# One decoder layer on one core: the written-out order of every engine and the engine of each free choice set anew

## The chip, the cores and the metric

The kernel runs on one core of a Trainium2 chip. The metric is device time in microseconds of one execution of the whole program, with all inputs and the output in HBM. A core has TensorE (PE in the profile; its weight loads are PEld), VectorE (DVE), ScalarE (ACT), GpSimd (POOL) and SyncE (SP), which here issues nearly all transfers. Each engine works through its own instructions in order; semaphores make one wait for another.

## The reference, cut to what matters

One layer of a decoder on a sequence of 512 tokens with 1024 channels, batch 1, all in float32:

```python
mod = silu(c) @ ada_w + ada_b                    # six rows of 1024: sh1, sc1, g1, sh2, sc2, g2
h = rms_norm(x, pre_norm_mix) * (1 + sc1) + sh1
z = h @ w_in                                     # g_rnn, x_rnn, q, k_c, v_c, k_s, v_s, k_w, v_w, gates
rnn = gelu(g_rnn) * rg_lru(causal_conv4(x_rnn))  # block-diagonal gates, then a scan over the tokens
att = nsa_attention(q, k.., v.., gates)          # compressed, selected and window parts, 8 heads, 2 KV groups
y = concat(rms_norm(rnn), rms_norm(att)) @ w_out
x = x + (1 + g1) * rms_norm(y, post_norm_mix)
h = rms_norm(x, pre_norm_mlp) * (1 + sc2) + sh2
y = square(relu(h @ w_ff1)) @ w_ff2              # 1024 -> 4096 -> 1024
x = x + (1 + g2) * rms_norm(y, post_norm_mlp)
```

## The kernel before

The float32 products are made of products of a shorter type: every operand is split into a high part (`hi`, a rounded copy) and a low part (`lo`, the operand minus `hi`), and three matmuls (hi x hi, lo x hi, hi x lo) are added up in PSUM. So each tile of weights takes, besides its load, a copy (`hi_a`, `hi_x`, `hi_g`, `hi_B`, `hi_e`, ...) and a subtraction (`lo_a`, ...) on ACT, DVE or POOL. The activations are split too (`h` and `h2l`, `fh` and `fl`).

The work goes in this order. First the four token tiles of `x` are normed and transposed, while the first sums of the modulation rows (`p<-p,silb`: a weight tile times the broadcast `silu(c)`, summed along the row) run on DVE. A first wave of projections makes keys, values and part of the rest. Then come the remaining projections, interleaved with the attention by blocks (scores `s`, masks and maxima `mx` on DVE, exponentials `p` on ACT, scaling by `den`, transposes `tp`, evacuation and split `pt`, products `pv`), with the recurrent block and with the projection out. From about 270 us on stands the MLP. Its first product (`up_pair`) and its second (`first_pair`, `second_pair`) use schemes in the manner of Strassen, with sums of weight tiles (`raw_A`, `raw_B`, `raw_D`) and of activations (`fS`, `fT`) ahead of the splits. The memsets of `K` (`zero`, L416) clear the half of each key tile that a head group does not use.

What sets the order is written out. While the program is built, every operation is a closure that the helpers `mm` (L340 in the profile), `turn` (L343), `act` (L350), `elem` (L384: DVE and POOL), `zero` (L416) and `load` (L430) append to a list of 5459 nodes. `flush` then sorts the list by a place for each node, two digits of the string `PLAN`, and calls it. So `PLAN` sets the order of each engine's queue and of SP's loads, and nothing else decides it. Where an operation can run on more than one engine (`copy`: ACT, DVE or POOL; `either`: DVE or POOL), a letter of `PLACE` (a, d, p) says which, taken in turn for each stream: XN norms of x, WS splits of weights and sums of weight tiles, AW after the first wave, AS scores, AV values, VW the recurrent block, FA end of the attention, RS residual, TH the transposed `h` of the MLP, UF and UP its first product, DN its second. There are 1056 letters.

```python
at = [b * DIGITS.index(PLAN[2 * k]) + DIGITS.index(PLAN[2 * k + 1]) for k in range(n)]
for k in sorted(range(n), key=at.__getitem__):
    self.nodes[k]()
...
ways = [w for w in ways if w[0][0] == PLACE[self.name][k]]
```

The tiles `fh` and `fl` of the second product lie in the pool `an` (L1687), in memory that the tiles of the pool `h2p` (`h2`, `h2l`, `s4h`) used before. Three neighbouring pools and `h2p` itself are opened with `reuse_waits="tile"`, `an` is not.

Of the kernel before, what the change touches and what calls it, by code (L numbers as in the profile page):

```python
# [14 lines left out]
P = 128  # L15
S = 512
D = 1024
# [48 lines left out]
    '&O&5&`&@&<&F&Q&J&f&U&=&G&p&M&l&e&H&N%z%d%y%u%{%}&+&9&4&L&0&>&]&v&[&o&g&q&R(-&b&{&h&t&S(/&c(#&k(F&T&P'
    '&7&K&.&C&E&I&_&X&i&,&D&m(1&s(%&x(H&z(;(2()&y(T(<(>(C(*&|(V(?#/(E(@(Q(L(.(3(8(=($(()%)*+2%X(|(h)2):(B'
    '(P(K(U(R(Y(a(~(G(6)3)9)>)U)b)y)^(m*2*8+l*d)/)C*A*K+d*o&a&*&u%q&V&Y(:&?(+&j(t&~)n(4)H(D*h(y*J)|*v*$+7'
    ')s+,*r+S+++x+&,<*),V,n#d#+#f#2$))?&d&n(&(5(7&w&r&}(,(W([#:#=#@#C#E#H#J#R#S#W#Y#[(9(A(I(j(Z(g(v#`#a#b'
    '#g#j#l#o#p(J(M(N#r#>#w$%#z(O(S(X(^(i(n(x(z({(})#)$)&)))0)Z)4)A)J*#*C+r/((](_(`(b(c(d(e(f(r)()M(k(l(o'  # L70
    '(p(q(s(u(w)G)Y)x)+),)-).)6)7)8)<)O)d)p)F)I)K)N)P)Q)R)S)W)v*+*5)a)e)h)1)5);)=)@)B)D)E)L)T)V)X)[)])_)c'
    ')j)o)t)w)z)~*%*(*F***4*t)`)f)g)i)k)l)m)q*T*]*y)r)u){)}*&*,*.*/*N*V+/*1*6*7*9*:*;*<*>*p+A+T*3*@*D*E*G'
    '*I*L*M*O*P*Q*S*U*W*X*Y*Z*_*`*b*c*i*j*k+:+)+L+G+E+[+o*a*l*m*w*x*{*|*}+#+i,4,>+0+4+8*[*^*e*-*0*?*=*H*B'
    '+?+F+M+N+|+u,),1*f*g*n*q*s*u*z*~+%+(+*+-+1+6+9+;+<+C+H+I+J+z,?,G,Z+Q+R+U+V+W+X+Y+]+`+b+e+h+k+m+n+s+t'
    '+v,,,6,8,;,=,C,F,M.P.q,Y,{-A.H+~,#,$*R+$-y.8,&,*,/,`,g-6/O,0,3,5,@,A,B,D,E,I,J,L,N,O,f,h,m,o,p,s,w,}'
    '-&+.+3+B+w+@,%+D+K+=+>+c+f+j,7+a+q-*-/-2-8-?-:-C->-1,P,R,S,U,[,b,c,e,j,k,l,q,r,t,u,v,x,y,z,|,~-#-$-%'
    '-+-J-P-V-(-)---.-0-3-5-7-9+O+P+^+}+Z,-+_,2-;-<-=+p+{,(,a,+,d,.,:-,-4-O-d-T-K-^-R-Y-@-B-D-E-H-M-N-Q-W'
    '-Z-c-q.$.5.:/&-F-S-U-]-b-m-I-L-X-f-_-`-e-h-j-l-u-x-|.t0%0K+g+y,T,i,Q,X.*.,.0,9,H,K-G.>.?.@.C.E.F/D/b'
    '/}.G.I.K.N.Q.`.e.k/>/M/80>0H#m.#.&.(.1.;.<.J.a.d-z.2.3.9.=.O-o-w.M.W,W,]-k-v-a-p,^,_-[-i.%.).x.{.4./'
    '...B.V.Z.].f.g.h/0/c/J-r-s.+.R.-.D-g-n-t-{.X.Y.b.c/%/..j.l.m.s/+/5.6.7._.i.[.n-}-~.A.U.v.|/_/#/F///g'  # L80
# [1813 lines left out]
```

## Time and profile before

| | |
|---|---|
| median of 3 runs | 605.06 us (604.8, 605.06, 607.66) |
| span of the profiled execution | 603.6 us; its own time is not listed |
| PE busy | 578.5 us, 96% of the span, 3424 matmuls |
| DVE busy | 562.5 us, 93%, 1148 instructions |
| ACT busy | 417.9 us, 69%, 848 |
| POOL busy | 193.7 us, 32%, 196 |
| chain that ended last | PE 75%, DVE 16%, ACT 4%, issue 2%, DMA 2% |
| HBM | 86.35 MB read, 2.10 MB written, 147 GB/s over the span |

The profile is of one execution. "L384 DVE" is an instruction that the helper at line 384 put on VectorE; since all share few lines, tiles are told apart by names: `out<-in`, with shapes behind. "x2" is a count; "[1.42 <-DVE mx L384]" is the idle time of the engine before an instruction and what ended it. Matmuls are pipelined and their ends are modelled, so a busy PE is not always at its rate.

### The profile page before, as it was taken

The numbers are of one execution on the slowest core, as the hardware profiler recorded it, in microseconds if no ns is written. First come the engines' busy times: TensorE is split into PE (matmuls) and PEld (weight loads), VectorE is DVE, ScalarE is ACT, GpSimd is POOL, SyncE is SP. The second block draws the span as 40 slices with busy tenths as digits, with TensorE's granted clock in tenths as the row PEclk, the third lists the DMA queues.
The fourth block names the chain that finished last, engine by engine and source line by source line (L and its number), as shares of the span: only waits on it lengthen the run. The fifth ranks groups of instructions, "written<-read, shape, count | busy, mean of one in ns | idle before, by whom it ended". The sixth has DMA issues, their size and how long they took to land.

```text
span 603.6 us, 9935 instructions
## 1 busy us (share of the span) xinstructions
PE 578.5 (96%) x3424; PEld 504.0 (84%) x3424; DVE 562.5 (93%) x1148; ACT 417.9 (69%) x848; POOL 193.7 (32%) x196
## 2 busy tenths in 40 slices
...
GB/s 347 416 377 372 280 283 181 36 75 100 6 275 175 71 47 61 1 105 71 71 141 140 72 140 73 138 130 189 222 54 151 128 157 122 147 168 123 121 1 139
DMA packets 26977, 89.08 MB, mean 148 GB/s; under 512 B 2992, under 2 KB 3504, under 8 KB 26928
## 3 DMA queue, kind: packets, MB, share of 16 engines
...
q14 instruction: 22, 0.18, 0.1%
...
HBM read 86.35 MB, written 2.10 MB: 147 GB/s over the span
## 4 chain that ended last, share of the span: by engine, by line
PE 75%; DVE 16%; ACT 4%; issue 2%; DMA 2%; POOL 0%; DVEq 0%; ACTq 0%
PE f L340 24%; PE pv L340 18%; PE s L340 17%; PE tp L340 11%; PE tp L343 4%; DVE r L384 4%; DVE p L384 3%; DVE fT L384 2%; DMA ar<-in_ada_r 1%; DVE raw_A L384 1%; DVE lo_c L384 1%; DVE lo_B L384 1%; ACT junk L350 1%; DMA vecs<-in_vecs 1%; DVE pt L384 1%
## 5 line engine op out<-in xcount | busy, mean ns | idle before, releaser
L350 ACT ACTIVATE p<-p,mx 128x32 f32<-128x32 f32 (+4 forms) x96 | 45.2, 473 | 10.2 <-DVE mx L384 10.1
L384 POOL TENSOR_SCALAR p<-p,den 128x32 f32<-128x32 f32 (+4 forms) x49 | 46.5, 964 | 13.6 <-DVE p L384 6.0
L340 PE MATMUL f<-hi_o,h 128*128 128x512 f32 x128 | 46.2, 410 | 0.2 <-ACT h L350 0.2
L350 ACT ACTIVATE hi_B<-raw_A 128x512 fp32r<-128x512 f32 x34 | 21.5, 633 | 29.1 <-DVE raw_A L384 14.9
L343 PE MATMUL tp<-ident,p 128*128 128x128 f32 x192 | 36.3, 273 | 1.1 <-DVE p L384 0.9
L340 PE MATMUL pv<-pt,V 128*128 128x256 f32 x160 | 36.8, 310 | 0.5 <-DVE pt L384 0.3
L384 DVE TENSOR_TENSOR pt<-tp,pt 128x512 fp32r<-128x512 f32 (+1 forms) x56 | 33.6, 609 | 3.6 <-ACT pt L350 2.1
L340 PE MATMUL s<-K,Q 128*128 128x288 f32 (+4 forms) x128 | 34.1, 330 | 1.4 <-DVE mx L384 1.4
L350 ACT ACTIVATE fT<-fT 128x512 f32<-128x512 f32 x52 | 31.5, 623 | 5.6 <-DVE fT L384 5.1
L384 DVE CUSTOM_DVE_ANT_0 p<-p,silb 128x1024 f32<-128x1024 f32 x24 | 31.2, 1308 | 0.1
L340 PEld LDWEIGHTS pv<-pt,V 128*128 128x128 f32 x160 | 26.2, 189 | 5.2 <-DVE pt L384 1.8
L350 ACT ACTIVATE pt<-tp 128x512 fp32r<-128x512 f32 (+1 forms) x47 | 25.3, 542 | 6.1 <-PE tp L343 4.2
L343 PEld LDWEIGHTS tp<-ident,p 128*128 128x128 f32 x192 | 24.3, 140 | 5.4 <-issue 1.7
L340 PEld LDWEIGHTS f<-hi_o,h 128*128 128x128 f32 x128 | 23.0, 188 | 4.1 <-ACT h L350 0.6
L340 PEld LDWEIGHTS s<-K,Q 128*128 128x128 f32 x128 | 22.2, 190 | 4.8 <-DVE mx L384 1.9
L340 PE MATMUL f<-lo_o,h 128*128 128x512 f32 x64 | 25.7, 403 | 0.0
L350 ACT ACTIVATE junk<-r 128x1024 bf16<-128x1024 f32 (+2 forms) x21 | 18.0, 856 | 10.7 <-DVE r L384 10.6
L340 PE MATMUL f<-third,hi_B 128*128 128x256 f32 x96 | 23.4, 283 | 0.9 <-DVE fT L384 0.9
L384 POOL TENSOR_TENSOR lo_e<-t,hi_e 128x512 fp32r<-128x512 f32 x1 | 1.3, 1297 | 67.4 <-ACT hi_e L350 67.4
L384 DVE TENSOR_TENSOR lo_B<-raw_A,hi_B 128x512 fp32r<-128x512 f32 x30 | 20.6, 687 | 2.4 <-ACT hi_B L350 0.9
L340 PE MATMUL f<-h,hi_g 128*128 128x512 f32 x64 | 22.5, 401 | 0.0
L340 PE MATMUL pv<-r,hi_B 128*128 128x256 f32 x96 | 22.2, 285 | 0.2 <-DVE fT L384 0.2
...
## 6 DMA issues: line engine op xcount, KB each, us to landing
...
```

Source lines behind the costliest of these rows:

```text
L340: lambda: self.nc.tensor.matmul(out, lhs, rhs, start=start, stop=stop))
L343: self.issue("pe", 0.109, [out], [src], lambda: self.nc.tensor.transpose(out, src, ident))
L350: return "act", cost, lambda: self.nc.scalar.activation(out, src, func, scale=scale, bias=bias, **kw), func
L384: return eng, cost, lambda: fn(out, *args, **kw), None
```

## The change

The set of operations is the same. The string `PLAN` is replaced as a whole (all queues and the loads get another order), 167 of the 1056 letters of `PLACE` differ, and the pool `an` gets `reuse_waits="tile"`, with which the first use of a tile waits for those older tiles that lay in its own memory, and not for the whole earlier pool. In the making of the new strings, an instruction of VectorE and one of GpSimd on SBUF were taken as excluding each other.

By letters: DVE to POOL 47, ACT to POOL 19, POOL to DVE 29, POOL to ACT 15, ACT to DVE 36, DVE to ACT 21. The core of the diff (`PLAN`, about 110 lines of digits, and the rows of `PLACE` for WS, UP and DN, 759 letters in all, of which 85 differ, are left out):

```diff
 PLACE = {'': 'aa',
-         'XN': 'aaadaaaaaaaa',
+         'XN': 'paaaaaaaaaaa',
...
-         'AW': 'aaaaaaaadpppadadddppadad',
-         'AS': 'papaaaappppaappppapappppdpaaddpaddpdpaaapapaapppppppaapappdpadapapaadadpppapappapppppppppppppadd'
-          'ppppapapdpaaapap',
-         'AV': 'aaaaaadaadadadaaaaaaadadadadaaaaaaaaaaaaaaaaaaaaaaadaaaa',
+         'AW': 'aaaaaaaaddppadadddppadad',
+         'AS': 'ddpaapappppppppdaapaadaapppapppppddpppaapappapppppapaaapdpaappppdadaaappppppdpappappdapdapppaapa'
+          'dpdppaadppapapap',
+         'AV': 'aadaaaaaddaaaaaaaadaadddddadadaaaaadaaaadaaaaaadaaadaaaa',
...
-         'FA': 'pppppdppdddp',
-         'RS': 'ppdppaddaddd',
-         'TH': 'aappaadddaddaaddaaddaaddaaddaadddaddaddaddaddddd',
-         'UF': 'adad',
+         'FA': 'ppppppppppdd',
+         'RS': 'pppppaddaddd',
+         'TH': 'aappaapddadddaddaappadddaappaadddaddaddaddaddddd',
+         'UF': 'addd',
...
-    an = ctx.enter_context(tc.tile_pool(name="an", bufs=1))
+    an = ctx.enter_context(tc.tile_pool(name="an", bufs=1, reuse_waits="tile"))
```

What the order does at the places spoken of below: the two evacuations `Q<-f,Q` that now stand behind sums `p<-p,silb` at 85 us stand ahead of three of them; the sum `ar<-ar,silb,ab` that is at 120.18 us in the trace goes 21 places back in DVE's queue, behind splits `pt`, and two `eg` go later; the two memsets of `K` leave the beginning of POOL's queue and stand around `lo_x` (one between `hi_x` and `lo_x`, one three instructions behind); the load of `raw_x` before them is issued three places earlier; a compressor weight's load goes from 12th to 35th; PE's eight products with `sil` come ahead of its ten warm-up products, of which four stood among them.

More of the change, by code (lines that the diff above doesn't have):

```diff
@@ L66 @@
[L66 to L80, printed above, removed]
@@ L166 @@
[L166 to L170 removed]
+    '#%#.#p#/#0#8#=#E#,#2#6#7#F#N#P#Q#S#e#L#M#O#R#d#*#(###$#&#)#+#b#U#c#x#K#T$$$%$&$($)$*$+$,$-#-#Y#Z#]$2'
@@ new lines @@
+    '$Y#5#^#_#g#i$[#V#`#a#h$5$8#f#n#v#{$7$h#t#o#q#y$:$.$/$0$1$4$3$6$>#w$<#z#|$;$I$F$k$H$N$R$J$G$l$Q$O$T$r'
+    '$i$m$j$o$V$?#~$#$`$=$K$L$P$U$W$X$a$9$A%9${$p$n$t$q$x$|$s$z$u$w$y%$$}%#$~%A%($B#}$@$_%7$D$E$M$S$]$^$e'
+    '$Z$d%Q%%%@%&%)%J%F%.%B%C%G%L%T%1%E%D%H%Y%U$C$b$c%6%5%+%-%/%0%2%3%<$g%;%P%Z%M%X%I%b%V%]%[%i%_%c%^%n%r'
+    '%p%m%o%a%=$f%:%O%8$v%*%,%K%R%S%e%4%>%N%s&?%x%q&<%k&8&D&5&6&>&;&9&G&7&:&E&@%?%f%h%j%l%t%u%y%{&)%z&&&/'
+    '&=&M&Q&B&F&A&L&O&R&C&X&N&[&Y&S&V&Z&P%|%d%g%W%`%v%w%~&$&+&%&-&k&s()&q&]&z&W&t(*&u&^(.&r&}(3&y&v(/(#&('
@@ new lines @@
+    '%}&,&H&I&J&K&U&`&d&#&*&l(+(E&{&w(0(,(-(F&|&x(D(1(4(K&~(((G(2#W(9(8(=(C(%($(:(5(6(7(|(Z,<&.(V(T)6)8(&'
+    '(?(;(S(A(B(X)#(<(>)&)()>)U)@)V(Y(U)A*B+Y*N*(.@*%*@+V*G&a&3&h&2&e&0&b&1&g&j)$&p)h):*D*+*K&n)W*,*M)}*I'
+    '*T+4*S+5*R+o+M,5-6,u-^#X,~#[*P&4))&T&c(H(I(J&i&_&f&m(@([#1#3#4#9#:#;#>#?#@#A#B#C(L(M(N(}(W(~)9#D#G#H'
+    '#I#J#j#k#l(O(P(Q#m#<#s+3#u(R(](^(_(`(a(b(c(d(e(f(g(j(p)+*&({)7);*E*J.9/A(h(i(k(l(m(n(o(q(z)%)<(r(s(t'
+    '(u(v(w(x(y)=)S)f)*)-)/)0)1)2)3)4)?)T)e)5)K)L)N)O)P)Q)R)X)d)g**)^)_)c),).)B)C)D)E)F)G)H)I)J)M)Y)Z)[)]'
@@ new lines @@
+    ')`)a)b)i)k)l)o)p)~*#*)*U)j)m)n)q)r)s)t)u*?*F*Q)v)w)x)y)z){)|*-*$*C+O*.*/*0*3*4*5*6*;*O+,+L*1*2*<*=*>'
+    '*V*W*X*Y*[*]*b*e*f*g*h*i*k*l*m*o*t*w*z*}*|+.+-+7+P,;*Z*j*n*q*r*s*u*v*{+_+s,>*~+#+6*9*:*^*7*8+8*A+T*H'
+    '+9+?+G+`,.,k,w,t*_*`*a*d*p*x*y+$+%+&+(+)+*+:+;+<+=+>+A+B+K+[,3,4,=+@+D+H+I+a+b+c+d+e+f+g+h+i+l+m+n+u'
+    '+v+w+z+{+|+}+~,,-#.2/|,9,:-Z-c+t+x+y*L+2.8.e,#,(,*,p,|.c/H,@,A,B,C,D,E,F,G,H,I,J,K,L,M,N,O,P,R,j,},l'
+    ',o*c+++1,m+0,0+/+Z+C+J+S,n+W,/+X,2,q,r,s,v-4,x,y-$,z,?,Q,S,T,U,W,X,Z,[,],_,`,a,b,c,d,e,f,g-&-.-/-0-1'
@@ new lines @@
+    '-3-9-L-]-:-<-=->-?-@-A-Q-R+E+F+R+^+U,-+Q+]-S-T-U+j+k+p,++r,1+q,{-5-7-8-E-e-F-C-D-f-V-i-j-k-l-n-q-t-u'
+    '-v-y-z.4.G.=/t-%-)-*-2-G-Y-(-;-K-b-m-o-}.#.%.&.-.../.[/I/},$,),6-H,8-I.0.H.I,%,&,7,i.J.K.L.M.N.O/G/s'
+    '/~.P.R.T.U.V.W.Z.d.Y0u.~0A3x#r-O-h.(.).+.,.7.D.a-x-{-|.*.E.F-p.$.?.^,^,h-,-J---N,V,Y-+-M-d-g.`/*.>.1'
+    '.5.3.X.f.g.p.v/#/-/=/J-B-X-`.6-_.A-P-W-[-a.o.q.r.s.{/(.h.i.u.w/+/@-w-~.:.B.<.C-r-s.;.].|.}/h/,/./0//'
+    '/C/4/9/:/;/1/6/D/F/</P/Q/T.Q.S.b/K._/M.j.k/)/f/[/]/e0t1y/R/V/Y/Z/d/r/W/X/^/k/x/y.t.x/?/a/>/B/7/8/E/L'
@@ new lines @@
+    '/u/v0r0p0&0%/w/z/o0)0+0500010?0@060D0F0G/_/g/O/b0H0I0]0l0j0E0J0K0N0b0s070M0O0P0a0y0*0:/p0$131415161&'
+    '1(1;1>1m1z1L1O1P1R1%1K1i1t0C0^2<2=2>2?2@2A2B3K440,0<1$1+1#1)0m0n101/0;/c0_0(0=090`.l.m.n0>121A11/$/%'
+    '/&1@0o0}0B/2/3/50q1F1E1B1D1e1}1d1f/N/S/U1I1J1_1g2L2h/`/i/j1|/l/m/n/q0-022I03040L080k3w1C.y.z0.0/0Q0R'
+    '0S0T0U0V0W0X0Y0Z0[0c0d0e0f0g0h0i0v0w0{0z0~1*0x0|3u1W1[1]1o21252627282;2O2P2Q2R2S2T2U2V2X2Y2_2`2a2b2p'
+    '2}3J3y171?1G1j1c1l1,1-1.1~18191:1M1N1Q1S1T1V1Y1Z1^1p2,2-1r1s1{2&1u2$1<1=1H1h2*2+2G3#2C2E2F2e2.2/201n'
@@ new lines @@
+    '1q1x2D1v2(1w2)2223241U1X1`2#1a2%1b1k2H2k2n3$4%3S3Q2~3U2s2t2x3]4{5&5h3+3,3-2W2Z2[2^2f2m2q2r2u2v2{3(35'
+    '36372N2]2i2y2l2z2j2|292:2K2c2J2d2M2g3%3)3*3O3R3[4y4i4>383;3<3A3B3F3H3I3`3a3b3d3e3h3i3m3n3o4#5V6D7A3&'
+    '3_3N4$3M3}3T4)3Y3p4&492w3.303:3Z3r3=3>3?3@3^3t3C3D3E3G3/333P3X4/4041434*4:3~4<4(4=4A4@4B4c4d4e4f4j4o'
+    '4p3{5f&o/{+N3q0#2o3|4I4M4z5W5^3k3l4-4.46484r4s4|5#34393L513V5A31323W5C4+4,424J4K4R4T4U4V4X4g4q524;4C'
+    '4E4F4Y4Z4[4G4N4`4a4k3z4h4l5X4n4L4O4S4W5b5i4~5,5n6q6+5(5)5*5+5B5`4w4}5.5a3f3g3s4?475@3c3j454x5Z5]5e6w'
@@ new lines @@
+    '5o5d6N5c4]4^4_4b4t4u5358595Q5R5S5t5u5z5{5|5}5~615s5w5y6%6,6#6$646:6G6?6@6C6L6K6&65686;6F6H4P4Q5/6/5-'
+    '5D6T6U6W6^6r6s4D4H4v5?6u6v7#7$7%54555E6a6h6i6j6X6Y6e6f6t6~56575<625=5k5F5I5J6y7?6A6p:/7&7)7+747(7*7-'
+    '7>5$5%50636E6I6J6M6}6|7L7M5M5N5O5P5T5U5l7J7R6{7O:.6=6P6Q6R6S6b6c6g6k767@7k8r77787=7]5K5L5Y6.5_5m6l6m'
+    '6n6z7_7`829,9*5:5;5>5j7B7W7Y7Z7m7n5x6(6667696<6V6[6]7U7V7a7b7o7p5q5v6)6-6*606_6`6d6x737C7X7[7^7f7x7y'
+    '7{5G5H5[6B6O6o8s8t7N7j887T8#8$8%868(8)8*8;7u7v7}7~858P8<8=8>8?7|8&8S8T6>6Z7/7K7.7H5p5r7,7I7071727579'
@@ new lines @@
+    '7:7q7t818A>S7D7E7g7h7i7w803v:-4m5g8O8V8z:>>R8C8D8G8L8X8[8^8b8c8k8v8u8W8Y8]8_8j8p8`8e8f8g8w9(7;7G7S7s'
+    '7Q7r7<7F7P7l8-8.8{9V878q838/8H8n8|9%90929S9l9o:q8K8d8h8~9K9a:,:2:F:H:I:J:V919394969#9&9?9C97989=9D7c'
+    '7e8@8M7d7z8,848+9F9J9Y9x:?9/95999;9@9O9H9I9L9R9]9`898:8B8N8E8F8Q8i9M9c9d9g9b9j9y9|9h9n:%:&8I8J8R8x8U'
+    '8Z8a8o8y9.9A9X9Z9B9W9[9U:*:+:7:A:@8}9$9-9v8l8m9+9>9)9r9~:#:$:6:=:0:3:4:5:9:S:Z:R:g:h:i9:9<9N9u9E9G9P'
+    ':8:K:N:O:]:C:E:L:M:[:p:b:d:e:m:^:_:`:a:j:s9Q9T9^9t9_9e9f9m9w:::X;/;|;.;-;3;M;#;2;J;[;D9s:;;K;L:u:x;$'
@@ new lines @@
+    ';%:w:y;I;O;&;9;;;Q9p9q9};,9i9k9{:Q9z:f:k:o:t:v:|:~;8;C;r<+<5<C:{;:;<;=;>;q<2<I<J;R;T;Z;^;c;d;l<-;p;@'
+    ';A;B;V;a;b:(:):<:P:1:G:W;0<e<f<u=+;f;g;h;i;m;o<Q<{<|<}=@=P;s;x;y;z;t;u;v;w;}</:B:D:T:Y:U:l:n:r;1;4;5'
+    '<W;_;{;H;P;X=k=m=r=t=u=v=}<&<(<)<*;~<#<$<%<0<1<,<6<7<8<3<4<<<D:c:z:};E;);*;6;G;7=w>(>)>*>+>,>->.>/>0'
+    '>1>2>9<9<@<A<K<L<S<T=<<d<=<><?<B<F<U<M<N<O<P<a<b;(;+;N<H;?;S;U<;<R<Y<_<g<Z<[<]<^<`<i<h<j<l<t<k<m<n<o'
+    '<r=*;W;e;n<:<.;j;k<E<G<V<c=5=&<q=%<s=(<v<w<x<~<y<z=$=,=#=-=2===>=B=^=a=`=.=/=0=1=;=E=?=A=C=D=F=H=G=I'
@@ new lines @@
+    '=N=O=J=K=L=M=R=Z=W=X=Y=[=S=T=U=V=_=b=]=d=f=g=c=e=h=i=l=n=o=p=q=s=x=z=y=|>#>4=~>$>3>8>W>Z>:><>[>7>F>Q'
+    '>6>G>T>]>c>d?/?Y@.?)@->e>g>m@/>n>o>p>~>C>D>^>_>`>a>|?$?|?~@I@J@N@i@K@M@k>b>f>h>i>j>l>};F;`<X;];Y<p=)'
+    '=4=6=Q=3=8=9=:=7=j={>%>&>5>=>A>B>E>J>P>O>N?0?1>;>>>?>@>M>H>K>L?2>y>k>q>u>x?*?,?(?%?9?:>r>s>t>w?-?+?#'
+    '?.?X?{>v?;?A?B?C?F?J?O?P?Q?[?a?b?j?k?l?n?o?p?q?v?w@<@C>I>U>V>Y>X?<?=?>???@?D?E?R?]?^?_?`>z>{?3?6?d?e'
+    '?f?g?h?r?t?u?x?y@1@U?s?z@%@&@(@*@+@0@2@4@5@6@7@@@A?}@B@D@W@X@Y@Z@q@s@v?&?4?5?8?7?T?i@Q@R@S@T@]@^@m?W'
@@ new lines @@
+    '?Z@$@)@n@t@u@x@z@{A$A%A?ATAUAZA]B,B@@,@8@9@:@;@F@G@H@E@L@w@3@=@>@?@d@e@O@P@lA4@_@`@a@b@h@f@g@cA3A2A)'
+    'A,A-A.A/AGA1A0A6AJA7A9ADA8AHAMAEAIALANAPB1A5AOB3B0@[@|A*A;A<A=ASA[A^A_A`AaAbAcAdAhAsAtAvAwAxAyB%B)@V'
+    '@o@p@rA(A:A>A@AAABAeAfAgAiAjAkArAuB&B(B+B-B.B/@y@}@~A#A&A+ACARAVAWAXAYAlAmAnAoApAzA{A|A}A~B#B$BABBBG'
+    'BHBIBJBKBVBWBZB[B]B_B`BaBbBdBeBhBkBlBmBnBq@#B4@jAFAKBrBsC.DKAQB5B2B6B:B=B9B>B;CUB7DADHOsB8C4CYCuCxCy'
+    'DJMbC/?G?H?I?K?L?M?N?S?U?V?c?mB<BMBTBYBcBfBgBiBjBtBvBwB|B?BEBFBLBNBOBPBSBUBXB^C,C2BQBRBuBxByBzB}C(C:'
@@ new lines @@
+    'C=CACHCZBoBpC#C$C&C*C+C<C?C@CBCGC[C^AqB*BCBDB{B~C%C>CCCDCECMCqCrCzDBC)CFCICJCKCNCOCPCQCRCSCTCpCsD@DC'
+    'G}C-C0C1C5C6C7CXC_C3CVC]CWCwCoCtCvC`CaDMDIC8C9C;CLCdCeCfCmD&D(D)D*DED+D,D6DPDoDpDqDrDsDtDvDwCbCcCnC{'
+    'C|C}C~D#D$D/D1D4DFCjCkD;DSDTDUDXDYDZD[D]D^DjCgChCiClD%D5D7D8D9D:D>D?DGD|D=DNDQDRDVD_D`DaDbDcDdDhDlD}'
+    'E,FfD-D.D0D2D3D<DODWDeDfDgDnE*E^F`FyM3DyE&E(E-E.E0E[EbE+E/EaDiDkEcEdEfDmDxF(F&E4E7E:E;E=E>E?EEEGEHEI'
+    'EKE]EFEJELEPEQEREUEVEWEXEYEZElEmEnEoEpErEtEvEwEzF#F%F)DuDzD{D~E#E$E%E)E1E2E5E6FBESETEqEsEuExEyE}F*F.'
```

160 lines of the change are left out of this document (57 added, 103 removed).

## The prediction

> **What bounds the kernel now.** I read the page's busy line and chain first, then TensorE's waits, then tables by stretch, and last the order of time around each wait.
>
> ```profile
> span 603.6 us, 9935 instructions
> PE 578.5 (96%) x3424; PEld 504.0 (84%) x3424; DVE 562.5 (93%) x1148; ACT 417.9 (69%) x848; POOL 193.7 (32%) x196
> PE 75%; DVE 16%; ACT 4%; issue 2%; DMA 2%; POOL 0%; DVEq 0%; ACTq 0%
> ```
>
> Two engines are nearly full: PE (TensorE) carries 75% of the chain that ended last, DVE (VectorE) 16%, POOL (GpSimd) 0%. The same matmuls run afterwards, so what an order can win is the time in which PE stands, or runs under its rate.
>
> ```profile
> PE s L340 <- DMA r<-in_x: 4.8, 1, 4.8
> PE s L340 <- ACT h L350: 1.8, 1, 1.8
> PE pv L340 <- DVE pt L384: 1.5, 2, 1.1
> ...
> PE s L340 <- ACT fh L350: 0.2, 1, 0.2
> ```
>
> After the first load (4.8, which no order removes) the waits are short and few (columns: total, times, longest); most of the others follow further down with the rows around them, and they are for DVE. Next, stretches: length, then busy time of PE, PEld, DVE, ACT and POOL, granted clock, DMA share, GB/s.
>
> ```profile
> 80.00:90.00 10.00, 8.27 (x46) 6.16 (x44) 9.75 (x18) 4.42 (x8) 9.84 (x3) 1.00 0.78 292
> 90.00:100.00 10.00, 9.33 (x41) 7.95 (x42) 8.70 (x30) 5.48 (x23) 1.04 (x2) 0.83 0.47 190
> 150.00:270.00 120.00, 118.66 (x723) 102.21 (x722) 112.04 (x313) 109.87 (x281) 84.50 (x93) 1.00 0.27 93
> 210.00:240.00 30.00, 30.00 (x201) 27.08 (x200) 28.39 (x103) 27.98 (x76) 23.75 (x30) 1.00 0.15 54
> 270.00:570.00 300.00, 298.36 (x1868) 268.94 (x1869) 288.55 (x498) 187.56 (x322) 47.98 (x40) 1.00 0.38 128
> 480.00:510.00 30.00, 30.00 (x134) 24.68 (x133) 29.83 (x47) 20.56 (x33) 0.00 (x0) 1.00 0.43 139
> ```
>
> From 270 to 570 PE idles 1.6 us of 300: what can be won lies ahead of that, where PE waits (80 to 90: 8.27 of 10) and where the clock drops behind a wait (0.83 from 90 to 100). Around four of the waits stand these rows.
>
> ```profile
> 80.07 3.77 POOL L384 TENSOR_SCALAR hi_x<-raw_x 128x1024 fp32r<-128x1024 f32 x1 [16.38 <-DMA raw_x<-in_wcol]
> ...
> 83.31 0.29 PE L340 MATMUL s<-K,Q 128*128 128x288 f32 x1
> ...
> 83.92 3.32 POOL L384 TENSOR_TENSOR lo_x<-raw_x,hi_x 128x1024 fp32r<-128x1024 f32 x1
> 84.92 3.40 DVE L384 CUSTOM_DVE_ANT_0 p<-p,silb 128x1024 f32<-128x1024 f32 x1
> 89.13 1.39 DVE L384 SCALAR_TENSOR_TENSOR Q<-f,Q 64x512 fp32r<-64x512 f32 x2
> 89.16 0.53 PE L340 MATMUL s<-K,Q 128*128 128x288 f32 x2 [1.42 <-DVE mx L384]
> 90.67 0.70 PE L340 MATMUL f<-h,hi_x 128*128 128x512 f32 x2 [0.99 <-DVE Q L384]
> ...
> 123.22 0.41 PE L343 MATMUL tp<-ident,p 128*128 128x128 f32 x2 [0.91 <-DVE p L384]
> 123.26 2.38 POOL L384 TENSOR_TENSOR lo_g<-raw_g,hi_g 128x1024 fp32r<-128x1024 f32 x1
> 123.40 2.27 DVE L384 TENSOR_SCALAR eg<-eg 128x24 f32<-128x24 f32 x1
> 126.72 0.38 PE L340 MATMUL pv<-pt,VC 128*128 128x256 f32 x1 [1.14 <-DVE pt L384]
> ...
> 268.51 3.10 POOL L384 TENSOR_SCALAR hi_f<-raw_f 128x1024 fp32r<-128x1024 f32 x1
> 268.88 1.60 DVE L384 TENSOR_TENSOR h2l<-h,h 128x256 fp32r<-128x256 f32 x2
> 270.20 0.39 PE L340 MATMUL pv<-h2l,hi_f 128*128 128x256 f32 x1 [0.34 <-DVE h2l L384]
> ...
> 403.14 1.30 POOL L384 TENSOR_TENSOR lo_B<-raw_B,hi_B 128x512 fp32r<-128x512 f32 x1 [8.44 <-ACT hi_B L350]
> 403.32 1.67 DVE L384 TENSOR_TENSOR raw_A<-raw_A,raw_B 128x512 f32<-128x512 f32 x1
> 405.93 0.35 PE L340 MATMUL f<-third,hi_B 128*128 128x256 f32 x1 [0.92 <-DVE fT L384]
> ```
> ```profile
> L384 DVE CUSTOM_DVE_ANT_0 p<-p,silb 128x1024 f32<-128x1024 f32 x24 | 31.2, 1308 | 0.1
> L384 DVE TENSOR_SCALAR eg<-eg 128x24 f32<-128x24 f32 x4 | 2.8, 708 | 0.1
> L384 DVE TENSOR_TENSOR lo_B<-raw_A,hi_B 128x512 fp32r<-128x512 f32 x30 | 20.6, 687 | 2.4 <-ACT hi_B L350 0.9 <-issue 0.4 <-PE pv L340 0.4
> L384 DVE TENSOR_TENSOR fl<-fS,fh 128x256 fp32r<-128x256 f32 x36 | 14.8, 417 | 0.0
> L384 POOL TENSOR_TENSOR lo_B<-raw_A,hi_B 128x512 fp32r<-128x512 f32 x6 | 8.1, 1348 | 19.4 <-ACT hi_B L350 19.4
> L384 POOL TENSOR_TENSOR fl<-fS,fh 128x256 fp32r<-128x256 f32 x4 | 4.8, 1192 | 18.1 <-ACT fh L350 18.1
> L384 POOL TENSOR_TENSOR fS<-fT,fT 128x256 f32<-128x256 f32 x4 | 3.3, 824 | 3.6 <-ACT fT L350 3.6
> L384 POOL TENSOR_SCALAR hi_g<-raw_g 128x1024 fp32r<-128x1024 f32 x1 | 2.8, 2767 | 0.0
> ```
>
> Each time a DVE instruction overstays beside a POOL instruction on SBUF: `p` 3.40 against a mean of 1.31, the 24 columns of `eg` 2.27 where the three others take (2.8 - 2.27) / 3 = 0.18, `raw_A` 1.67 against 0.69 for a row of its size. `eg` ends at 125.67 with POOL's `lo_g` at 125.64. So POOL shuts DVE out, but not always: from 210 to 240 DVE is busy 28.39 and POOL 23.75 of 30, where DVE mostly reads scores in PSUM.
>
> **The change part by part.** The diff adds and removes no operation; engine letters at 167 of 1056 choices and the whole order differ, and one pool's waits. So I compared the two orders of each queue.
>
> *80 to 100.* Now two sums `p` stand in DVE's queue ahead of both `Q` evacuations, so one `p` held by `lo_x` makes PE wait 1.42 + 0.99. In the new order both `Q` stand ahead of three sums. The wait goes: 2.4. The clock at 0.83 for 10 us costs 10 x 0.17 = 1.7, and goes with it if the idle caused it (from 0 to 1.7; I take 1.7, as the stretch before it stood at 1.00). Late next: the first maxima `mx`, one instruction behind `Q`.
>
> *120 to 127.* The sum `ar` at the head of this group moves 21 places back, behind the `pt` splits, and `eg` back too; the waits 0.91 and 1.14 go: 2.05. Against it, three copies `hi_g` come to POOL, 2.77 each, and one `hi_v`; that is within the +29 below.
>
> *270 and 406.* That `hi_f` leaves POOL: 0.34. That `lo_B` leaves POOL for DVE, 0.69 there, which is less than the hold of 0.98; the wait 0.92 may go or be met by its own `lo_B`: half, 0.46.
>
> *The beginning.*
>
> ```profile
> 4.65 1.25 POOL L416 MEMSET K<- 64x1056 f32 x1
> 5.11 0.82 DVE L384 TENSOR_SCALAR sil<-sil 128x8 f32<-128x8 f32 x1
> ```
>
> The two `K` memsets leave the head of POOL's queue, so `sil`, 8 columns, can take what the 24 of `eg` take, 0.18: 0.64 earlier. All eight silb matmuls come before the ten warm-up matmuls, but PE's first real matmul waits 1.8 for ACT's `h`, whose norm also waits for the fourth tile. From 0 to 1.0; I take 0.7. The `K` memsets don't vanish: one now stands between `hi_x` and `lo_x`. `hi_x` waits for its load and ends at 83.84; with 1.25 behind it the memset ends at 85.1, and scores from that `K` began at 83.31. So the cost is 0 to 1.8. The load of `raw_x` is issued three places earlier, ahead of two of 512 KB, which at 292 GB/s take 1.8 each; so I take 0.5, for `lo_x` coming later too.
>
> *`reuse_waits`.* The pool of `fh`/`fl` then waits for the tiles it overlays one by one. ACT's `fh` waits for matmuls now, and PE for `fh` 0.2: from 0 to 0.6, as ACT has 31% free; I take 0.3.
>
> *Engine letters.* 66 instructions come to POOL and 44 leave it. At the mean of the nearest row each: 256 wide with two inputs 21 in, 8 out, at 0.82 to 1.19 (+11 at 0.86, as `fS` is the commoner); 512 wide with two inputs 11 in, 5 out, at 1.35 (+8); 1024 wide copies 5 in, 2 out, at 2.77 (+8); 1024 wide with two inputs 2 in, 1 out, at 2.38 (+2); softmax scalings and other small work 27 in, 28 out, about even. Net +29 on 193.7. DVE gets 65 and gives 68: -2.9. ACT: -11.5, off the path with 31% idle. Of POOL's +29, 11 fall in 270 to 420 and 11 behind it, where DVE gives 1.6 and 5.0.
>
> What do the added 29 cost? POOL has room; DVE may be held. The four rows above lose 2.1 + 2.1 + 0.8 + 1.0 = 6.0 on DVE for 193.7 of POOL, so 29 at that rate lose 0.9. From -0.9 (new pairs all better placed) to all 29 held; I take double the rate, 1.8, since most lands where DVE is fullest, and 0.5 more for waits that a shuffled PE order opens at places with none now.
>
> *Queues.* SP's loads: the first eleven stand almost as before, one compressor weight goes from 12th to 35th. At 512 KB each and 292 GB/s, 35 loads take 63 us, so it is there before the scores at 83.31, and its product is formed beside them. PE's order moves by seven places on average; ACT's table loads keep their number and sequence.
>
> Sum: 2.4 + 1.7 + 2.05 + 0.34 + 0.46 + 0.7 + 0.3 = 7.95, less 0.5 + 1.8 + 0.5 = 2.8, leaves 5.15. The span goes from 603.6 to 598.5. The median before, 605.06, is 1.46 above that span (runs 604.8 to 607.66; the profiled execution's own time isn't given), so I forecast 605.06 - 5.15 = **599.9**. A difference under 0.5% (3 us) a measurement of this kernel can't tell from none.
>
> The Trainium skill, "SBUF — State Buffer", section "Who interferes with whom", says that a VectorE instruction with two SBUF inputs, or in a two-port mode, and a GpSimd instruction that reads SBUF exclude each other for a whole instruction, and that the one issued first decides. The ends of `eg` and `lo_g` within 0.03 agree; so do the PSUM readers from 210 to 240. By the page every added POOL instruction beside DVE's two-input splits is a hold, which speaks against the new letters: it would give the third rival's 609 in place of my 599.9.
>
> **The rivals.**
>
> *No change (602 to 608).* The holds move to other places and PE, 96% busy, keeps its pace: the 7.95 come back as other short waits. For it: PE is at 30.00 of 30 in the quietest stretches; the six waits are 1% of the span. Against: each is a DVE instruction standing ahead of one that PE needs, and the diff swaps just these. About 605.
>
> *More (590 to 596).* PE also gets denser from 150 to 270, where it counts as busy but isn't at its rate. In 480 to 510, 134 matmuls of 512 columns fill 30.00: 0.224 each. The stretch holds about 267 of 512 columns, 50 of 288 to 416, 212 of 256 and 178 transposes, taken at half a product of 512 as two at 123.22 took 0.41 in all (counts by the operations' shapes): 59.8 + 7.1 + 23.7 + 19.6 + 1 = 111, so 9 of 120 are slack. Half of that besides: 605 - 7.95 - 4.5, near 593. Against: ACT is busy 109.87 and DVE 112.04 of 120 there, so little is loose.
>
> *Slower (608 to 614).* From 270 on, POOL takes DVE one for one. POOL gets +22, DVE gives 6.6, so DVE's need grows by 15.4; it idles 300 - 288.55 = 11.45 from 270 to 570. Its surplus is 4: 609, and with half the idle usable 15.4 - 5.7 = 9.7: 615. It decides once held time exceeds the idle. For it: DVE at 29.83 of 30 with POOL at 0.00, in 480 to 510, on splits from SBUF to SBUF. Against: POOL's 48 in this stretch now cost PE little (1.6 idle), and a hold of DVE costs PE only where no buffer is full.
>
> **How the numbers follow.** Forecast (596 to 602) 0.45; more 0.13; no change 0.22; slower 0.20. Faster by over 0.5% is forecast and more: 0.58; within it 0.22; slower 0.20. The range leaves out under 2 in 10: down to 591 (most of "more"), up to 609.5 (the first end of "slower"). The forecast's own range is 596 to 602.
>
> **What would show it.** Right: PE's waits for `mx`, `Q`, `p`, `pt` gone between 85 and 127, granted clock 1.00 from 90 to 100, no `eg` or `p` over 2 us on DVE; POOL near 223; PE's first wave matmul half a microsecond or so earlier. Wrong: new PE waits for `fT`, `fl` or `lo_B` behind 270, DVE means of these rows above 0.69 and 0.42 (the slower rival); the same waits at other names with the span kept (no change); PE busy from 150 to 270 done in 115 or less (more).

## The result and the profile after

The changed kernel takes 608.81 us (median of 4 runs, 608.33 to 610.33) against 604.93: a ratio of 1.0063, 95% interval 1.0041 to 1.0085. It is slower by about 3.9 us, where 5.15 less was forecast. It still lies in the range given (591 to 609.5), whose upper end was set by the slower rival. The profiled execution took 610.33, with a span of 608.5; so its trace shows about 1 us more of the loss than the medians do.

The page's lines that answer to those of before:

```profile
span 608.5 us, 9959 instructions
PE 582.6 (96%) x3424; PEld 503.2 (83%) x3424; DVE 565.0 (93%) x1145; ACT 411.1 (68%) x829; POOL 228.0 (37%) x218
PE 61%; DVE 24%; issue 6%; DMA 4%; ACT 3%; POOL 1%; DVEq 0%; SPq 0%; ACTq 0%; POOLq 0%
```

POOL rose by 34 us (29 were worked out), and DVE's share of the chain from 16% to 24%. Where the time went is seen best by following TensorE's work. Each matmul is given the spacing it has when nothing stops it (in these traces 0.227 us for 512 columns, 0.119 for 256, and so on), and both traces are asked when they reach the same sum. The lag is the difference; below zero the changed kernel is ahead. It is good to about half a microsecond, and to one between 80 and 170 us, where it depends on how the small shapes are weighted.

```
TensorE's work done, us     10    20    40    60    80   110   130   170   230   260   300   340   430   534
reached before, at us     24.5  35.2  56.1  77.7 103.3 143.6 166.5 211.9 285.2 315.3 356.1 397.7 489.9 593.9
lag of the changed one    -2.7  -2.4  -1.2  +1.3  +1.1  -1.8  -0.2  -1.3  -0.2  +1.4  +2.4  +4.1  +5.1  +5.3
```

So it leads after the beginning, has lost the lead by 78 us, leads again at 144, and loses 5.3 us from 285 to 490 (5.5 to the end). One trace is one execution, though. Five more traces below have the changed kernel's order and letters up to 280 us: their lag is -0.8 to +0.2 at 78 us (here +1.3) and -2.3 to -1.6 at 285 us (here -0.2). So about 1.4 to 2.1 us of what this trace lost ahead of the MLP is its own; the loss in the MLP comes back in others (5.6 us in after_lo_x, 7.3 in old_then_new). The changed kernel's tables by stretch (busy time of PE, PEld, DVE, ACT, POOL, clock, DMA share, GB/s):

```profile
46.00:80.00 34.00, 30.81 (x161) 25.16 (x160) 31.73 (x43) 26.19 (x39) 5.56 (x6) 1.00 0.83 304
80.00:90.00 10.00, 8.08 (x42) 6.11 (x41) 9.89 (x19) 2.27 (x5) 5.17 (x3) 1.00 0.92 345
90.00:100.00 10.00, 9.32 (x49) 7.30 (x48) 9.59 (x31) 5.78 (x17) 6.40 (x4) 1.00 0.59 218
120.00:130.00 10.00, 10.00 (x50) 7.27 (x49) 8.30 (x24) 8.80 (x25) 8.60 (x7) 1.00 0.19 62
270.00:480.00 210.00, 207.38 (x1452) 191.56 (x1451) 200.71 (x350) 127.31 (x220) 55.77 (x44) 1.00 0.37 123
```

Three of these stretches in the kernel before:

```profile
46.00:80.00 34.00, 33.40 (x177) 28.24 (x176) 32.33 (x48) 28.57 (x43) 3.91 (x6) 1.00 0.84 315
120.00:130.00 10.00, 7.75 (x45) 5.93 (x44) 9.39 (x20) 5.79 (x18) 5.67 (x5) 1.00 0.33 107
270.00:480.00 210.00, 208.36 (x1472) 194.73 (x1473) 201.23 (x365) 134.34 (x237) 38.65 (x32) 1.00 0.36 122
```

In the last of them, 270 to 480, POOL has 17 us more in the changed kernel, DVE is as busy though it issues 15 instructions fewer, and PE gets through 20 matmuls fewer. A row of time shows how. This is the changed kernel at 397 us:

```profile
397.17 1.73 POOL L384 TENSOR_TENSOR lo_C<-raw_A,hi_C 128x512 fp32r<-128x512 f32 x1 [0.97 <-ACT hi_C L350]
397.66 1.51 DVE L384 TENSOR_TENSOR fT<-fT 128x256 f32<-128x256 f32 x1
399.10 0.41 DVE L384 TENSOR_TENSOR fT<-s,fT 128x256 f32<-128x256 f32 x1
...
400.55 0.50 PE L340 MATMUL pv<-r,hi_B 128*128 128x256 f32 x2 [0.69 <-DVE fT L384]
```

`fT<-fT`, with both inputs in SBUF, takes 1.51 instead of 0.42 and ends 0.27 behind POOL's `lo_C` (399.17 and 398.90), which itself began beside a split on DVE and took 1.73 instead of about 1.3; the evacuations queue behind `fT`, and TensorE waits for the last of them. I add up such overstay: duration less what the quickest quarter of instructions of the same form take. From 270 to 480 it is 2.7 us on DVE before and 11.3 after.

Little of this shows in the list of TensorE's waits, which adds up to 1.8 us in this stretch before and 2.2 after: a matmul's modelled length covers a short pause. The pauses are in the spacing. What consecutive matmuls are apart beyond their quickest spacing adds up, between the same two amounts of work (285 to 490 us before, 285 to 495 after), to 5.2 us before and 10.5 after, in many small pieces.

### The profile page after: what moved, and what is told of

It is laid out like the page before. It is cut to its first block, busy times and chain, and to the rows that moved or that the text cites. A ratio compares the mean times of both kernels' runs of the same rounds, so it can differ in the third digit from the quotient of the medians.

```text
span 608.5 us, 9959 instructions
## 1 busy us (share of the span) xinstructions
PE 582.6 (96%) x3424; PEld 503.2 (83%) x3424; DVE 565.0 (93%) x1145; ACT 411.1 (68%) x829; POOL 228.0 (37%) x218
## 4 chain that ended last, share of the span: by engine, by line
PE 61%; DVE 24%; issue 6%; DMA 4%; ACT 3%; POOL 1%; DVEq 0%; SPq 0%; ACTq 0%; POOLq 0%
PE f L340 20%; PE pv L340 14%; PE s L340 13%; PE tp L340 10%; DVE p L384 6%; PE tp L343 4%; DVE r L384 3%; DVE fT L384 2%; DMA raw_c<-in_wc 2%; DVE lo_B L384 1%; DVE fl L384 1%; DVE raw_A L384 1%; DVE lo_D L384 1%; DMA p<-in_ada_t 1%; DVE pt L384 1%
## 5 line engine op out<-in xcount | busy, mean ns | idle before, releaser
L340 PE MATMUL s<-K,Q 128*128 128x288 f32 (+4 forms) x128 | 36.2, 338 | 3.4 <-DVE K L384 1.9
L343 PE MATMUL tp<-ident,p 128*128 128x128 f32 x192 | 37.9, 275 | 0.8 <-POOL p L384 0.5
L384 POOL TENSOR_TENSOR fl<-fS,fh 128x256 fp32r<-128x256 f32 x5 | 6.8, 1357 | 81.4 <-DVE raw_D L384 52.6
L350 ACT ACTIVATE fT<-fT 128x512 f32<-128x512 f32 x48 | 28.9, 621 | 5.3 <-DVE fT L384 5.0
L343 PEld LDWEIGHTS tp<-ident,p 128*128 128x128 f32 x192 | 24.6, 140 | 6.9 <-DVE pt L384 1.2
L350 ACT ACTIVATE pt<-tp 128x512 fp32r<-128x512 f32 (+1 forms) x41 | 22.0, 540 | 4.5 <-PE pv L340 3.0
L350 ACT ACTIVATE fh<-fS 128x256 fp32r<-128x256 f32 x39 | 15.3, 409 | 13.9 <-DVE fS L384 7.2
L350 ACT ACTIVATE hi_D<-raw_d 128x1024 fp32r<-128x1024 f32 x14 | 14.8, 1058 | 12.9 <-PE f L340 5.3
L350 ACT ACTIVATE hi_e<-raw_e 128x1024 fp32r<-128x1024 f32 x14 | 14.8, 1056 | 12.6 <-PE pv L340 6.2
```

Source lines behind the costliest of these rows:

```text
L340: lambda: self.nc.tensor.matmul(out, lhs, rhs, start=start, stop=stop))
L343: self.issue("pe", 0.109, [out], [src], lambda: self.nc.tensor.transpose(out, src, ident))
L350: return "act", cost, lambda: self.nc.scalar.activation(out, src, func, scale=scale, bias=bias, **kw), func
L384: return eng, cost, lambda: fn(out, *args, **kw), None
```

## The experiments

The theory, A: GpSimd's reads of SBUF hold VectorE in the MLP (the prediction's slower rival). The rival, B: the new order of the MLP is looser by itself. A third, C: the loss comes from ahead of the MLP, or from `reuse_waits`.

Orders can be joined: take the nodes that one order has up to a place, in that order, and the rest in the other's, each with its letters. In the kernels of the runs the helpers stand on other lines than in the two kernels: L333 or L339 for `mm`, L343 or L349 for `act`, L377 or L383 for `elem`.

**Where it is.**

```diff
 new_then_old:  PLAN/PLACE of the change for its first 2630 nodes, of before for the rest; an without reuse_waits
 old_then_new:  PLAN/PLACE of before for its first 2641 nodes, of the change for the rest; an with reuse_waits
```

> The new order and letters up to where TensorE stands at about 283 us (2630 nodes), the order and letters of the kernel before behind it, without reuse_waits. If the loss lies in the MLP (A and B alike): about 604, as the lag at 283 us was -0.2 to -1.0 us. If the loss comes from ahead of it and is only seen later (theory C: buffers and loads put behind by the attention's order): 607 or more.

> The mirror image: order and letters of the kernel before up to about 283 us (2641 nodes), the new ones behind it, with reuse_waits. A and B: 605 + 5 to 6 = 609 to 611. C: 604 to 606.

Measured: new_then_old 603.61 (ratio 0.9972, 0.9954 to 0.9989), old_then_new 610.58 (1.0109, 1.0083 to 1.0134). In the traces new_then_old keeps a lead of 2.3 from 285 us to the end, and old_then_new goes from a lead of 1.6, with the old order up to there, to a lag of 5.7. The whole loss, and more, is in the MLP; C is out as far as it means the attention's order.

**reuse_waits.**

```diff
 no_reuse (on the changed kernel) / before_reuse (on the kernel before)
-    an = ctx.enter_context(tc.tile_pool(name="an", bufs=1, reuse_waits="tile"))
+    an = ctx.enter_context(tc.tile_pool(name="an", bufs=1))        # no_reuse; the reverse in before_reuse
```

> The changed kernel without reuse_waits on the pool of fh and fl. From the prediction's term (0 to 0.6 us gained by it): 608.8 to 609.4. If the finer waits were what costs the new order time: 607 or less.

> The kernel before with reuse_waits on the pool of fh and fl alone. The prediction's term: 0 to 0.6 us faster, 604.4 to 605. The new order without it lost 8.5 us, because it puts uses of that pool ahead of the last reads of what lay there; if the old order has the same need hidden, it would gain more than 1 us.

Measured: no_reuse 617.33 (1.0207, 1.0184 to 1.023), before_reuse 605.58 (1.0008, 0.9996 to 1.0019). The finer waits change nothing in the old order and are worth 8.5 us in the new one. The longest wait of TensorE in the MLP of no_reuse, and the row of ACT that it comes from:

```profile
PE f L333 <- ACT last L343: 6.7, 1, 6.7
```
```profile
440.20 1.15 ACT L343 ACTIVATE fh<-fT 128x512 fp32r<-128x512 f32 x2 [9.20 <-PE f L333]
```

`fh` is the first tile in `an`. ACT waits 9.20 with it for matmuls `f` of the MLP's first product, which read what lay in that memory; `last`, an evacuation of the first product, stands behind it in ACT's queue, and TensorE waits for `last`. In the changed kernel the same `fh` begins at 432.70, 0.1 us behind the instruction ahead of it, and TensorE has no such wait. Both expectations missed.

**The engine letters in the MLP.**

```diff
 mlp_letters_back: order of the change, all 78 letters that differ behind its node 2630 as before
 after_mlp_p2d:    order of the change, of these only the 28 from DVE to POOL as before
```

> The changed kernel with its whole order, and with the engine letters of the kernel before for all 78 choices that differ from about 280 us on (28 go from GpSimd back to VectorE, 14 from VectorE to GpSimd, the rest between ScalarE and VectorE). Between the two profiles the lag of TensorE behind the kernel before grows by about 6 us from 283 to 500 us. Theory A (GpSimd's added instructions hold VectorE there; VectorE's overstay from 270 to 480 rose from about 3 to 11 us): the lag of this stretch falls by 4 us or more, to some 604 to 605 in all. Theory B (the new order of the MLP is itself looser, whatever the engines): 608 to 609, no more than 1 us better than the changed kernel, or worse.

> The changed kernel with only those 28 choices taken back, from about 280 us on, that it gave from VectorE to GpSimd. VectorE gets some 28 x 0.42 to 0.69, about 14 us, more to do and loses about 8 us of overstay, with about 10 us idle from 270 to 480. If the added GpSimd work is a loss by itself: 605 to 608. If the order needs VectorE's room at those places, even at the price of the holds: 610 to 616.

Measured: 632.97 (1.0475, 1.0448 to 1.0502) and 628.29 (1.0382, 1.0363 to 1.0402). Both are far above what was expected. They don't tell A from B, as I had thought the first would: an order and its letters belong together. In after_mlp_p2d the overstay fell to 7.2 us, and the time rose by 20; TensorE waits 4.0 for `last` and 3.7 for `fh`, which it doesn't in the changed kernel. I take it that DVE's instructions stand in its queue at places where POOL was to have done them beside it; no run shows this apart. Within this order the moves to POOL save more than the holds cost.

**The reads alone.** Order and letters stay; GpSimd's 55 late instructions with a choice of engine become memsets of their outputs, in after_memset_dep led by the real operation on 8 columns. These kernels leave those sums, splits and copies out of the computation.

```diff
+    part()                                  # after_memset_dep only: the operation on [:, :8]
+    nc.gpsimd.memset(out, 0.0)              # 3 or 4 times (2 or 3 behind part)
-    fn(out, *args, **kw)
```

> The changed kernel, in which the 55 GpSimd instructions with a free choice of engine from about 280 us on are replaced by three or four memsets of the same output, about as long together, that read nothing (this leaves their sums, splits and copies out of the computation). Order, engines and all other instructions stay. Theory A (GpSimd's reads of SBUF hold VectorE): VectorE's overstay from 270 to 480 falls from 11.7 us to 4 or less, and TensorE's lag from there on shrinks by 4 to 6: 602 to 605. Theory B (the new order of the MLP costs by itself, because of how VectorE's, ScalarE's and TensorE's instructions follow each other): 607 to 609.

> The same replacement in the kernel before (40 instructions from about 280 us on; their sums, splits and copies are left out of the computation). Its overstay from 270 to 480 is 3.1 us and TensorE idles 0.9 us there behind such a one, so A and B: 603.5 to 605.

> As after_memset_mlp (the sums, splits and copies of the 55 late GpSimd instructions are left out of the computation), but each begins with its own operation on the first 8 columns, so that it waits for its inputs as before; two or three memsets follow. Theory A (the reads hold VectorE): 604.5 to 606, as without the waits (605.2), overstay from 270 to 480 at 4 us or less. If the gain there came from results that were ready sooner: 607 to 609.

Measured: after_memset_mlp 605.19 (1.0004, 0.9991 to 1.0017), after_memset_dep 604.69 (0.9991, 0.9976 to 1.0006), and before_memset_mlp 605.03 (0.9997, 0.9979 to 1.0014). The changed kernel gains 3.6 and 4.1 us when GpSimd is as busy but does not read wide; the kernel before gains nothing. Results that are ready sooner are not the reason, since after_memset_dep waits for its inputs. Its stretch, and the place of above:

```profile
270.00:480.00 210.00, 208.69 (x1459) 193.73 (x1458) 196.49 (x357) 130.42 (x224) 58.16 (x132) 1.00 0.37 126
```
```profile
393.83 0.64 POOL L387 TENSOR_TENSOR lo_C<-raw_A,hi_C 128x8 fp32r<-128x8 f32 x1 [0.90 <-ACT hi_C L350]
394.33 0.42 DVE L384 TENSOR_TENSOR fT<-fT 128x256 f32<-128x256 f32 x1
394.53 1.11 POOL L292 MEMSET lo_C<- 128x512 f32 x2
394.67 0.41 DVE L384 TENSOR_TENSOR fT<-s,fT 128x256 f32<-128x256 f32 x1
```

POOL is busy 58.2 us here, more than in the changed kernel, and DVE works through 7 instructions more in 4.2 us less. The overstay is 3.2. `fT` takes 0.42 beside the memset. In the trace the MLP still loses 1.7 us (lag -2.1 at 285 us, -0.4 at the end) of the 5.5: that rest is the order's, or of what the memsets changed besides; I did not part them. So A carries most of the loss, B at most the rest.

**The dose, on the old order.**

```diff
     fn(out, *args, **kw)                                               # each of 40 late POOL operations
+    nc.gpsimd.tensor_tensor(tab[:, :n], silb[:, :n], silb[:, 512:512 + n], op=add)    # before_reads
+    nc.gpsimd.memset(tab[:, :n], 0.0)                                  # before_writes, 3 or 4 times
```

> The kernel before with one more GpSimd instruction behind each of its 40 late ones (from about 280 us on): a sum of two tiles in SBUF that nothing needs, of the same width up to 512, written to a mask that is no longer used. It adds some 45 us of GpSimd, off every chain. Theory A (reads on GpSimd hold VectorE): VectorE's overstay from 270 us on grows by 6 us or more over the 6.3 of now, and the time by 2 to 6 us, to 607 to 611. Theory B (the order alone): 604.5 to 605.5.

> The control: the same places, three or four memsets of that mask instead, about as long and reading nothing. Theory A as far as it rests on reads: VectorE's overstay and the time stay, 604.5 to 605.5. If any use of SBUF by GpSimd holds VectorE: as before_reads.

Measured: before_reads 630.49 (1.0419, 1.0392 to 1.0446), before_writes 616.54 (1.0195, 1.0171 to 1.022). Both are far above what was expected. The control costs 11.6 us without a read: the memsets stand in POOL's queue ahead of its next real instruction, and TensorE waits 3.3 us for results of POOL, which it did not before. One of its new waits in before_writes, and one in before_reads:

```profile
PE pv L339 <- POOL lo_C L383: 1.7, 1, 1.7
```
```profile
PE s L339 <- DVE lo_C L383: 2.7, 3, 1.3
```

The reads cost 14 us more than the memsets at the same places, and DVE's overstay from 270 to 480 goes to 26.1 us (10.6 with the memsets, where each of the eleven DVE instructions that overstay by over 0.15 us lies beside a real operation of POOL, none beside memsets alone). A row of before_reads:

```profile
327.34 1.74 POOL L291 TENSOR_TENSOR tab<-silb 128x512 f32<-128x512 f32 x1
327.85 1.78 DVE L383 TENSOR_TENSOR raw_A<-raw_A,raw_B 128x512 f32<-128x512 f32 x1
```

Beside the sum that nothing needs `raw_A` (0.69 elsewhere) lasts 1.78.

**The first step by itself.**

```diff
 q_ahead: order of before, with the nodes
-    ... ACT Q, p (sum), mx, mx, Q, mx, Q
+    ... ACT Q, Q, Q, p (sum), mx, mx, mx          in VectorE's queue at 85 us
```

> The kernel before with three nodes moved: the two evacuations Q that stand behind a sum p in VectorE's queue at 85 us are put ahead of that sum (which GpSimd's lo_x holds). This is the first step of the prediction by itself: the waits of 1.42 and 0.99 us and the clock of 0.83 behind them go, 2.4 to 4.1 us: 601 to 602.5. If another wait takes their place, as in the changed kernel, where TensorE waits 1.92 for a K evacuation behind a held r: 604 to 605.

Measured: 603.34 (0.9983, 0.9966 to 1.0), so hardly clear of no change and between the two expectations, and a lead of 1.8 us at 114 us in its trace. Its rows:

```profile
90.00:100.00 10.00, 9.65 (x54) 7.97 (x54) 9.56 (x38) 6.94 (x26) 2.32 (x2) 1.00 0.60 234
```
```profile
89.24 0.53 PE L333 MATMUL s<-K,Q 128*128 128x288 f32 x2 [1.44 <-DVE mx L377]
```

The wait for `Q` is gone, and the clock from 90 to 100 is 1.00 instead of 0.83. The wait for `mx` is there as before.

But the clock can't all be put down to the move, for the drop comes and goes with one and the same order. Six traces have the old order up to 270 us (before, before_reuse, before_reads, before_writes, before_memset_mlp, old_then_new). Three show the drop between 88 and 96 us (in before_reads and before_reuse twice as long as in before), and three stay at 1.00, with the waits for `mx` and `Q` in place. before_writes:

```profile
15.00:20.00 5.00, 3.26 (x17) 2.51 (x17) 5.00 (x11) 4.31 (x9) 0.00 (x0) 1.00 1.03 406
90.00:100.00 10.00, 9.16 (x49) 7.84 (x50) 9.18 (x34) 6.20 (x25) 1.43 (x2) 1.00 0.53 205
```

The three without it are 1.0 to 1.1 us ahead of the trace of before at 114 us. That is the price of before's drop there (the two with the longer one are 0.7 behind it), and it leaves 0.7 to 0.8 of q_ahead's lead for the move itself. Of 76 executions of the kernel before beside which the runs were timed, 35 have a mean clock of 0.990 or less, with a median of 605.46, and 33 of 0.993 or more, with 604.61; of q_ahead's 12 none is under 0.991. So the move may well make the drop rarer; one trace can't show it.

> The changed kernel with one letter different: the lo_x that GpSimd runs at 82.55 us, under which VectorE's r overstays by 2.1 us, runs on VectorE (about 1.2 us). If that hold makes TensorE wait 1.92 us for K: the wait falls to 1 us or less, and TensorE's lag at about 92 us from +0.7 to about -0.3. If it is K's place behind the sums: the wait stays at 1.9 or grows. In the total no more than 1 us, 607.8 to 609.

```diff
 after_lo_x: the changed kernel, the one letter of this lo_x: p -> d
```

Measured: 607.97 (1.0036, 1.0021 to 1.0051), less than the changed kernel's 608.81 by 0.8, as expected. In its trace the wait for `K` is gone, which stands, 1.6 to 2.1 us long, in all seven traces that have the hold: the hold made it. The lag at 92 us is -2.1 (the changed kernel's +0.7; I had expected -0.3), but this trace is of an execution of 605.47, 2.5 under its median, and had 1.4 of the difference already at 78 us. The rows, first of the changed kernel, then of this one:

```profile
82.55 2.62 POOL L384 TENSOR_TENSOR lo_x<-raw_x,hi_x 128x1024 fp32r<-128x1024 f32 x1
82.83 2.62 DVE L384 TENSOR_SCALAR r<-r,vecs 128x512 f32<-128x512 f32 x1
85.37 1.21 DVE L384 CUSTOM_DVE_ANT_0 p<-p,silb 128x1024 f32<-128x1024 f32 x1
86.62 0.69 DVE L384 TENSOR_TENSOR K<-pv,K 64x512 fp32r<-64x512 f32 x1
87.46 0.37 PE L340 MATMUL s<-K,Q 128*128 128x288 f32 x1 [1.92 <-DVE K L384]
```
```profile
81.54 0.55 DVE L377 TENSOR_SCALAR r<-r,vecs 128x512 f32<-128x512 f32 x1
82.00 1.22 DVE L377 CUSTOM_DVE_ANT_0 p<-p,silb 128x1024 f32<-128x1024 f32 x1
83.26 0.69 DVE L377 TENSOR_TENSOR K<-pv,K 64x512 fp32r<-64x512 f32 x1
83.99 1.23 DVE L377 TENSOR_TENSOR lo_x<-raw_x,hi_x 128x1024 fp32r<-128x1024 f32 x1
```

**A version that beats both.**

```diff
 mix4: order and letters of the change for its first 240 nodes, of before up to its node 614, of the change up to its node 2630, of before to the end
 mix5: as mix4, back to before at the change's node 1180 (about 143 us); both without reuse_waits
```

> Four pieces: the new order and letters up to about 35 us (240 nodes), the old ones to about 80 us, the new ones to about 283 us, the old ones behind. Theory O (in the stretch from 46 to 80 us the new order is the slower one; it gave back 3 us of lead there): the lead is kept, and with the 2.3 of new_then_old this makes some 599.5 to 600.5. Theory D (this stretch is bound by VectorE's work and the loads, whatever the order, and any lead is spent waiting for them): 601.5 to 603.6, as new_then_old.

> As mix4, but back to the old order and letters at about 143 us (1180 nodes) instead of 283. In mix4 TensorE's lead was 7.1 us at 143 us and 5.1 at 285. If that loss lies in the new order of this stretch, 600 or less, 1 to 2 us ahead of mix4; if the lead can't be kept there because the stretch is bound by ScalarE and VectorE whatever the order, 601 to 602.

Measured: mix4 601.50 (0.9952, 0.9936 to 0.9968), mix5 600.06 (0.9916, 0.9896 to 0.9936). mix5 holds its lead of 7 us from 143 us to the end. Of the lead of 2.7 at 24 us, mix4 had 1.0 left at 78 us, with the old order in between: neither O nor D alone. Both kernels then gain some 2.2 us from 78 to 92 us, and 3.6 by 100 us, where the old stretch leads into the new one and no wait for `K` or `Q` stands in the trace; about 1.0 of it is the drop of the clock in the trace of before.

## Why the prediction was wrong

Point by point, by its own steps.

- *80 to 100 (2.4 + 1.7).* Half right in mechanism, nothing in the sum. `Q` did go ahead of the sums, but `lo_x` now held the `r` that stands ahead of the `K` evacuations, and TensorE waited 1.92 there; a later sum `p` took 3.00 beside `lo_v` at 91.19. I named `mx` as late next; I had not asked which instruction would next stand beside `lo_x`. By itself the move brought about 1.5 us at most (q_ahead): of the 1.42 for `mx` nothing came, since the maxima stand behind the held sum too. The 1.7 for the clock took one execution's drop for the order's. It is in half of the traces of the old order, worth 1.0 to 1.8 us where it is, and three of eight traces with the new order have a drop from 86 to 91 us as well (new_then_old and both memset runs on the changed kernel).
- *120 to 127 (2.05).* Right: PE is busy 10.00 of 10 from 120 to 130 (7.75 before), and the lag falls by 2 to 3 us from 103 to 144 us.
- *270 and 406 (0.8).* The 0.34 at 270 went. Wrong at 406: TensorE still waits for `fT`, before (the first two rows) and in the changed kernel (the last):

```profile
PE f L340 <- DVE fT L384: 0.9, 1, 0.9
PE pv L340 <- DVE fT L384: 0.2, 1, 0.2
```
```profile
PE pv L340 <- DVE fT L384: 1.2, 3, 0.7
```

- *The beginning (0.7).* The sign was right, the size too small: the lead is 2.7 at 24.5 us. TensorE's first product of the wave came 1.0 earlier (14.70 against 15.71), and TensorE is then busy 5.00 us of 5 from 15 to 20. The clock before was 0.68 in these 5 us:

```profile
15.00:20.00 5.00, 4.29 (x16) 3.50 (x17) 5.00 (x11) 4.31 (x9) 0.00 (x0) 0.68 1.03 414
```

5 x 0.32 = 1.6 looks like the rest of the lead, but it isn't. Three of the six traces of the old order have no drop there (before_writes above), and they are only 0.1 to 0.2 us ahead of the trace of before at 35 us: before_writes is busy 3.26 of the 5 us and waits 0.99 for DVE's `h`. So the rest is the new order's, which leaves TensorE no such wait. The lead was then spent by 78 us in the changed kernel's trace (PE 30.81 of 34 busy from 46 to 80, 33.40 before), and nearly or wholly in its siblings, which no term of mine had. Of the 0.5 set against this for the memsets of `K`, no wait of TensorE for one is in the trace.
- *reuse_waits (0.3).* Priced in the old order, where it is worth nothing; the new order loses 8.5 us without it. A term for a wait has to be asked of the order that will run.
- *Engine letters and the +29 us of POOL (-2.3).* This is the step that failed and made the sign wrong: the cost of the holds, put at 1.8, with 0.5 more for new waits. The mechanism was named in the slower rival and its price, 4, is what after_memset_dep gives back (4.1). I took a rate of overstay for each us of POOL from four rows over the whole kernel, 0.03, and doubled it; all of DVE's overstay before, 23 us, would have made it 0.12. Where the 17 us came, sums and splits with two inputs in SBUF are about 163 of DVE's 201 us (from 90 to 270 us they are some 22), and 8.6 us of overstay came with them: 0.5 for each us. The rival's signs came too, if faintly: DVE's mean for `fl<-fS,fh` went from 0.417 to 0.449, for `fT<-fT` of 256 columns from 0.420 to 0.556. The rival's condition was wrong too: DVE still idles 9.3 us from 270 to 480. The holds cost TensorE before that idle was used up; in the row at 397 us one falls on a DVE instruction that a product waits behind, and I take the others to be alike.

So the first 283 us brought 1.3 us (new_then_old) of the 6.7 hoped for there (7.95 less 0.46 and 0.3, which lie behind, and less 0.5), and the MLP took 5 or so. Pieces of the new order among the old, in mix5, bring nearly 5. That 608.81 lies in the range is no merit of the forecast, 596 to 602: the range took in the first end of the slower rival, which had 0.20. The Trainium skill, "SBUF — State Buffer", section "Who interferes with whom", says that a VectorE instruction with two SBUF inputs contends with a GpSimd instruction that reads SBUF, not with one that only writes it. The runs agree: 1.51 beside `lo_C`, 0.42 beside its memset, and 11.3 against 3.2 us of overstay.
